# Score matmuls over all 128 rows, scratch in operand order, and fewer transfers in a two-layer encoder on one core

## The chip, the core and the metric

The kernel runs on one NeuronCore of one Trainium2 chip. The metric is the device time of one execution in microseconds. The kernel before takes 1938.34 us in the median of three runs (1934.69 to 1938.78). TensorE (PE) multiplies, its weight loads are shown as a row of their own (PEld), VectorE is DVE, ScalarE is ACT, GpSimd is POOL, and SyncE (SP) issues nearly all DMA transfers.

## What is computed

Two layers over 512 tokens of 1024 channels, in float32. Each layer has a mixer and a gated feed-forward part, each between two RMS norms:

```python
h = rms_norm(x, norm_mix_pre[l], NORM_EPS)
z = h @ w_in                                  # all q, k, v and the gates
# differential attention: 4 heads of two 64-wide score halves
s = einsum('bqhcd,bkhcd->bhcqk', qblk, kk) * scale
p = softmax(s); a = p[:, :, 0] - lam_full * p[:, :, 1]
o = einsum('bhqk,bkhe->bqhe', a, v)           # v is 128 wide
# three groups of 8 heads, window and dilation (128,1), (512,4), (2048,16)
og, lg = dilated_window_attention(qg, kg, vg, dilation, side)
ob = sum over groups of softmax(lse) * og
m = (sigmoid(g_A) * (oa @ w_a) + sigmoid(g_B) * (ob @ w_b)) @ w_out
x = x + rms_norm(m, ...); x = x + rms_norm(swiglu(rms_norm(x, ...)), ...)
```

q and k are rotated (rotary embedding over the two 32-wide halves of a 64-wide head) before the scores.

## The kernel before, in words

Activations are kept channel by token: `hT` holds the normed input as eight blocks of 128 channels by 512 tokens. Every float32 product is made of three matmuls of a rounded type: each operand is split into a high part and the rest (`mm3`, lines 123 to 125: high x high, low x high, high x low). Weights come in pieces of 1 MB (`load_raw`, line 90), two buffers of them; ACT rounds them (line 108) and DVE takes the rest (line 109).

TensorE's order is written out by hand. Projections are generators (`ws_gen`, `proj_v`) that give way after twelve matmuls over 512 columns, or 24 over 256; at each such point `att_step` emits one step of the attention work that is due. `attq` holds this work as a queue; a part is pushed when its projections are done, with a delay in steps (`DELAY`: 4 for the differential part, 7 for its first half; 4 for the first group, 2 for the others), and starts when the part ahead of it has issued its last scores. The heads of a layer are worked on in two halves (u = 0 and 1): first the differential part of both halves, then for each half the three dilated groups, then the gates and the output products. A step of attention has scores, some steps later transposes (line 521 or 646), and then products with v (line 532, 662 or 664), each for another item.

q and k leave the projection with the first rotary halves of four heads in one tile and the second halves in another, since the rotation needs them on the same rows. Scores need the 64 channels of a head on 64 rows. So `qk_split` writes the high and low parts to a scratch in DRAM (`dasc`) and reads them back in pieces of 32 rows. The three products of the high and low parts are two matmuls: QX holds for each head q's high part on 64 rows and its low part on the other 64 (which half is which alternates with the head), KX has k's high part twice, and KL k's low part, with two heads side by side on 128 rows:

```python
b = 64 * (c % 2)
nc.tensor.matmul(o, QX[:, c, qs], KX[:, c, ks], start=True, stop=False)
nc.tensor.matmul(o, QX[b:b + 64, c, qs], KL[b:b + 64, c // 2, ks], start=False, stop=True)
```

The second of them (line 488) works on 64 rows. The differential part and the first group use these two (512 and 256 columns); the second and third group take plain float32 operands from another scratch (`gsc`) with 64-row matmuls (line 616). The first group also moves v through DRAM (`vd`), because its windows need the tokens in natural order while the kernel keeps them by residue classes of 16; its result goes back through `scr` and `scs`. At the kernel's two ends x is read and written in that class order.

The transfers of q, k and v are all issued by SP, in one queue with the weight loads; an entry that waits holds up those behind it. `big` tiles (8 KB a row) have seven buffers, `m4` tiles eight.

Of the kernel before, what the change touches and what calls it, by code (L numbers as in the profile page):

```python
# [9 lines left out]
F32 = mybir.dt.float32  # L10
# [11 lines left out]
MOVE_POOL = 0  # L22
# [12 lines left out]
def encoder_trunk_kernel(  # L35
# [9 lines left out]
    mv = [0]  # L45
# [183 lines left out]
    def rows_in(xt, src, n, permuted):  # L229
        if permuted:  # L230
            for s in range(4):
                nc.sync.dma_start(out=xt[32 * s:32 * s + 32, :], in_=class_rows(src, n)[s])
        else:
            nc.sync.dma_start(out=xt, in_=src[n * P:(n + 1) * P, :])
# [17 lines left out]
    def postnorm_tile(n, pe, src, g, dst, src_perm, dst_perm):  # L252
# [12 lines left out]
        if dst_perm:  # L265
            for s in range(4):
                (nc.gpsimd if s == 3 else nc.sync).dma_start(out=class_rows(dst, n)[s], in_=xt[32 * s:32 * s + 32, :])
        else:
            nc.sync.dma_start(out=dst[n * P:(n + 1) * P, :], in_=xt)
# [51 lines left out]
    def specs():  # L321
# [11 lines left out]
        for l in range(depth):  # L333
            for u in range(2):
                yield from qkv(l, 256 * u, 512 + 256 * u, 1024 + 256 * u)[(1 if l == 0 and u == 0 else 0):]
            for u in range(2):
                for gi in range(3):
                    b = GB + gi * 1536 + 256 * u
                    yield from qkv(l, b, b + 512, b + 1024)
# [48 lines left out]
    for l in range(depth):  # L388
# [34 lines left out]
        def move(dst, src):  # L423
            mv[0] += 1
            eng = nc.gpsimd if MOVE_POOL and mv[0] % MOVE_POOL == 0 else nc.sync
            eng.dma_start(out=dst.bitcast(F32) if dst.dtype == F32R else dst,
                              in_=src.bitcast(F32) if src.dtype == F32R else src)

        def big(shape=(P, 4, S), dt=F32R):
            return ap.tile(list(shape), dt, tag="big", name=nm("big"), bufs=7)  # L430
# [25 lines left out]
        def qk_split(natural, first=None):  # L456
            QX, KX = big(), big()
            KL = m4([P, 2, S], F32R)
            sc = dp.tile([P, 2, 2, 2, S], F32, tag="dasc", name=nm("dasc"), bufs=2)
            for which in range(2):  # L460
                pair = rope((yield from proj_qk(which, first)), natural)
                hi = rt(F32R)
                nc.scalar.copy(out=hi, in_=pair)
                lo = rt(F32R)
                nc.vector.tensor_tensor(out=lo, in0=pair, in1=hi.bitcast(F32), op=ALU.subtract)
                move(sc[:, which, 0], hi)
                move(sc[:, which, 1], lo)
                src = sc.rearrange("(c j) w hl ab t -> w hl ab j c t", j=32)[which]
                if which == 0:
                    for hl in range(2):  # L470
# [429 lines left out]
```

## Time and profile before

| | |
|---|---|
| median of 3 runs | 1938.34 us |
| the profiled execution's own time | 1938.61 us |
| its span, first to last instruction | 1936.8 us |
| TensorE clock granted, mean | 0.994 |
| TensorE busy | 1889.4 us, 98% |
| weight loads busy | 1586.0 us, 82% |
| DVE, ACT, POOL busy | 929.5, 671.5, 179.9 us |
| DMA | 244.92 MB, 126 GB/s over the span |

A group row of the profile gives line, engine, operation, output<-inputs, shape and count, then busy time and mean duration, then the engine's idle time ahead of such instructions and what ended it. A time-line row starts with its start and its length in us, and in brackets stands the idle time before it with what ended it. A windows row gives the stretch, its length, the busy time of PE, PEld, DVE, ACT and POOL with their instructions, the granted TensorE clock, and DMA's busy share with GB/s. A transfer row gives the KB of each and the median us from issue to landing. The stages lie in time as follows: layer 0 has its differential scores from 79 us and its dilated groups until about 430 us, layer 1 the same from 1034 us and until about 1400 us; feed-forward parts lie behind each.

### The profile page before, as it was taken

Reading aid. Unit: us, or ns where it says so; the run is one execution under the profiler, and the core shown is the slowest. Engines: PE = TensorE matmul, PEld = TensorE weight load, DVE = VectorE, ACT = ScalarE, POOL = GpSimd, SP = SyncE. Lnnn points to the kernel's source line nnn. Section 1 sums busy time; section 2 is a strip of 40 time slices with the busy share of each in tenths; the row PEclk is TensorE's granted clock in tenths of the full one; section 3 lists DMA queues with packets and bytes.
Section 4 is the critical chain, followed back from the end, with each engine's and each line's share of the span. In section 5 each row is a group of like instructions: output and inputs, shape, how many; then the busy total and the mean of one; then the engine's idle time right before and its main releaser. Section 6 shows DMA issues by size and latency. Waiting matters only on the chain. (4 is left out here: it accounts for less than half of the span.)

```text
span 1936.8 us, 24393 instructions
## 1 busy us (share of the span) xinstructions
PE 1889.4 (98%) x9952; PEld 1586.0 (82%) x9952; DVE 929.5 (48%) x1243; ACT 671.5 (35%) x1301; POOL 179.9 (9%) x136
## 2 busy tenths in 40 slices
PE   6999999999999999999999999999999999999997
PEld 6878887888888888888887788878888888888886
DVE  4676556544545333332366765556453453333222
ACT  3354333344224322221334544323432342222221
POOL 1111013011100000000011211121100000000000
PEclk9999999999999999999999999999999999999999
DMA  6844446442244332322448254554323432323232
GB/s 176 253 127 131 121 120 185 129 121 87 87 163 153 109 109 87 103 94 88 162 151 233 88 151 120 151 162 130 100 89 137 144 131 89 107 87 109 87 119 65
DMA packets 171871, 244.92 MB, mean 126 GB/s; under 512 B 10864, under 2 KB 136176, under 8 KB 171760
## 3 DMA queue, kind: packets, MB, share of 16 engines
q1 hardware_dynamic: 171568, 242.84, 41.2%
q8 instruction: 78, 1.28, 0.3%
q0 software_dynamic: 192, 0.52, 0.1%
q14 instruction: 33, 0.27, 0.0%
HBM read 205.52 MB, written 37.81 MB: 126 GB/s over the span
## 5 line engine op out<-in xcount | busy, mean ns | idle before, releaser
L123 PE MATMUL pj<-hTh,whi 128*128 128x512 f32 (+1 forms) x1600 | 610.1, 381 | 3.0 <-ACT hTh L248 3.0
L124 PE MATMUL pj<-hTl,whi 128*128 128x512 f32 (+1 forms) x1600 | 600.2, 375 | 6.0 <-DVE hTl L249 5.9
L125 PE MATMUL pj<-hTh,wlo 128*128 128x512 f32 (+1 forms) x1600 | 599.6, 375 | 0.0
L109 DVE TENSOR_TENSOR wlo<-raw,whi 128x1024 fp32r<-128x1024 f32 x252 | 341.1, 1355 | 489.4 <-ACT whi L108 480.4
L108 ACT CAST whi<-raw 128x1024 fp32r<-128x1024 f32 x252 | 264.7, 1051 | 771.2 <-PE pj L124 498.6
L123 PEld LDWEIGHTS pj<-hTh,whi 128*128 128x128 f32 x1600 | 304.0, 190 | 62.7 <-ACT hTh L248 5.2
L124 PEld LDWEIGHTS pj<-hTl,whi 128*128 128x128 f32 x1600 | 304.3, 190 | 58.0 <-DVE hTl L249 7.7
L125 PEld LDWEIGHTS pj<-hTh,wlo 128*128 128x128 f32 x1600 | 304.1, 190 | 54.6
L123 PE MATMUL pj<-whi,hTh 128*128 128x256 f32 x512 | 148.5, 290 | 0.0
L125 PE MATMUL pj<-whi,hTl 128*128 128x256 f32 x512 | 144.8, 283 | 0.0
L124 PE MATMUL pj<-wlo,hTh 128*128 128x256 f32 x512 | 144.8, 283 | 0.0
L634 ACT ACTIVATE e<-e,gst 128x128 f32<-128x128 f32 (+1 forms) x192 | 81.9, 428 | 140.0 <-DVE gst L631 139.9
L77 POOL TENSOR_TENSOR sm<-sm,mhalf 128x1 f32<-128x1 f32 (+1 forms) x48 | 28.7, 599 | 970.1 <-DVE sm L75 970.1
L123 PEld LDWEIGHTS pj<-whi,hTh 128*128 128x128 f32 x512 | 97.9, 191 | 6.0 <-issue 3.7
L124 PEld LDWEIGHTS pj<-wlo,hTh 128*128 128x128 f32 x512 | 98.0, 191 | 0.0
L125 PEld LDWEIGHTS pj<-whi,hTl 128*128 128x128 f32 x512 | 98.0, 191 | 0.0
L825 DVE TENSOR_TENSOR s<-s,pj 128x512 f32<-128x512 f32 x44 | 30.3, 689 | 123.7 <-PE pj L125 123.6
L420 POOL TENSOR_TENSOR r<-r,r 128x512 f32<-128x512 f32 x32 | 43.0, 1344 | 453.3 <-DVE r L418 332.8
L418 DVE TENSOR_TENSOR r<-pj,cos 128x512 f32<-128x512 f32 x48 | 32.9, 690 | 77.4 <-PE pj L125 77.4
L419 POOL TENSOR_TENSOR r<-r,r 128x512 f32<-128x512 f32 x32 | 64.5, 2015 | 25.0 <-DVE r L418 25.0
L487 PE MATMUL at<-big,big 128*128 128x256 f32 (+1 forms) x128 | 55.3, 432 | 9.6 <-DMA vd<-m 7.5
L287 PE MATMUL pj<-whi,ac 128*128 128x512 f32 x160 | 63.0, 394 | 0.0
(166 smaller groups left out, 2482.0 us busy)
## 6 DMA issues: line engine op xcount, KB each, us to landing
raw<-in_w_in_dram SPq DMA_DIRECT2D x64, 1024.0 KB, 7.0
raw<-in_w_gate_up_dram SPq DMA_DIRECT2D x44, 1024.0 KB, 5.1
raw<-in_w_down_dram SPq DMA_DIRECT2D x22, 1024.0 KB, 4.8
dasc<-r SPq DMA_DIRECT2D x32, 512.0 KB, 3.5
big<-dasc SPq DMA_DIRECT2D x64, 128.0 KB, 6.6
big<-dasc SPq DMA_DIRECT2D x32, 256.0 KB, 8.0
gsc<-r SPq DMA_DIRECT2D x16, 512.0 KB, 3.5
big<-gsc SPq DMA_DIRECT2D x32, 256.0 KB, 7.3
```

Source lines behind the costliest of these rows:

```text
L108: nc.scalar.copy(out=shp(hi), in_=src)
L109: nc.vector.tensor_tensor(out=shp(lo), in0=src, in1=shp(hi.bitcast(F32)), op=ALU.subtract)
L123: nc.tensor.matmul(o, ah, bh, start=(i == 0), stop=False)
L124: nc.tensor.matmul(o, ah, bl, start=False, stop=False)
L125: nc.tensor.matmul(o, al, bh, start=False, stop=(i == n - 1))
L287: nc.tensor.matmul(o, al, hi[:, sl], start=False, stop=False)
L418: nc.vector.tensor_tensor(out=dst[:, i], in0=u, in1=tb, op=ALU.mult)
L419: nc.gpsimd.tensor_tensor(out=pair[:, 0], in0=pair[:, 0], in1=tmp[:, 0], op=ALU.subtract)
L420: nc.gpsimd.tensor_tensor(out=pair[:, 1], in0=pair[:, 1], in1=tmp[:, 1], op=ALU.add)
L487: nc.tensor.matmul(o, QX[:, c, qs], KX[:, c, ks], start=True, stop=False)
L634: nc.scalar.activation(out=e[:, i, :], in_=e[:, i, :], func=AF.Exp, bias=sts[:, n, h:h + 1], accum_out=sts[:, n, 4 + h:5 + h])
L825: nc.vector.tensor_tensor(out=s, in0=s, in1=ou_[i], op=ALU.mult)
```

## The change

- The low part of k gets a layout of its own, KL, over 128 rows. The scratch `dasc` now holds one of q or k with rows in the order (high or low, rotary half, channel), four heads beside each other, so that one read of 128 rows x 8 KB gives QX, one gives KH (high above low), and two of 64 rows give KL, the same halves swapped. Both score matmuls then use all 128 rows: QX x KH gives high x high and low x low, QX x KL the two mixed products. So a fourth product, low x low, is computed that was left out before.
- Each of q and k is written by four transfers of 256 KB and read by one (q) or three (k), where two writes and eight reads stood. The scratch has three buffers instead of two, `big` eight instead of seven.
- In the first group the order of the projections is k, v, q instead of q, k, v (the weight stream's order with it); the differential part and the other groups keep q, k, v.
- In the other two groups q's and k's halves are read back apart, each by one transfer; `vd`, `scr`, `scs`, the x rows at the start and the output rows at the end go by one transfer in place of four. The last output rows are all issued by SP; POOL had one in four.
- The number of score matmuls, their columns and the attention steps are as before. The DMA scratch space for POOL's transfers is set to 4096 bytes.

```diff
@@ -227,11 +225,7 @@
         return t.rearrange("(t s r) c -> r s t c", s=4, r=4)[n]
 
     def rows_in(xt, src, n, permuted):
-        if permuted:
-            for s in range(4):
-                nc.sync.dma_start(out=xt[32 * s:32 * s + 32, :], in_=class_rows(src, n)[s])
-        else:
-            nc.sync.dma_start(out=xt, in_=src[n * P:(n + 1) * P, :])
+        nc.sync.dma_start(out=xt, in_=class_rows(src, n) if permuted else src[n * P:(n + 1) * P, :])
 
     def prenorm_scale(xt, t, g):
         ss = small(1)
@@ -262,11 +256,7 @@
         nc.vector.tensor_tensor(out=ss, in0=ss2[:, 0:1], in1=ss2[:, 1:2], op=ALU.add)
         r = rstd_of(ss, 1, 1.0 / D, NORM_EPS)
         nc.vector.scalar_tensor_tensor(out=xt, in0=t, scalar=r, in1=xt, op0=ALU.mult, op1=ALU.add)
-        if dst_perm:
-            for s in range(4):
-                (nc.gpsimd if s == 3 else nc.sync).dma_start(out=class_rows(dst, n)[s], in_=xt[32 * s:32 * s + 32, :])
-        else:
-            nc.sync.dma_start(out=dst[n * P:(n + 1) * P, :], in_=xt)
+        nc.sync.dma_start(out=class_rows(dst, n) if dst_perm else dst[n * P:(n + 1) * P, :], in_=xt)
         return xt, t
 
     def new_hT():
@@ -336,7 +326,8 @@
             for u in range(2):
                 for gi in range(3):
                     b = GB + gi * 1536 + 256 * u
-                    yield from qkv(l, b, b + 512, b + 1024)
+                    q, k, v = qkv(l, b, b + 512, b + 1024)
+                    yield from (k, v, q) if gi == 0 else (q, k, v)
 
             def gates(c):
                 return [win(l, ZC + 256 * c, "cols"), win(l, ZC + D + 256 * c, "cols")]
@@ -421,13 +412,11 @@
             return pair
 
         def move(dst, src):
-            mv[0] += 1
-            eng = nc.gpsimd if MOVE_POOL and mv[0] % MOVE_POOL == 0 else nc.sync
-            eng.dma_start(out=dst.bitcast(F32) if dst.dtype == F32R else dst,
+            nc.sync.dma_start(out=dst.bitcast(F32) if dst.dtype == F32R else dst,
                               in_=src.bitcast(F32) if src.dtype == F32R else src)
 
         def big(shape=(P, 4, S), dt=F32R):
-            return ap.tile(list(shape), dt, tag="big", name=nm("big"), bufs=7)
+            return ap.tile(list(shape), dt, tag="big", name=nm("big"), bufs=8)
 
         oaT = [big() for i in range(2)]
 
@@ -453,43 +442,33 @@
                 nc.scalar.copy(out=v[:, 2 * n2:2 * n2 + 2, :], in_=o)
             return v
 
-        def qk_split(natural, first=None):
-            QX, KX = big(), big()
-            KL = m4([P, 2, S], F32R)
-            sc = dp.tile([P, 2, 2, 2, S], F32, tag="dasc", name=nm("dasc"), bufs=2)
-            for which in range(2):
-                pair = rope((yield from proj_qk(which, first)), natural)
-                hi = rt(F32R)
-                nc.scalar.copy(out=hi, in_=pair)
-                lo = rt(F32R)
-                nc.vector.tensor_tensor(out=lo, in0=pair, in1=hi.bitcast(F32), op=ALU.subtract)
-                move(sc[:, which, 0], hi)
-                move(sc[:, which, 1], lo)
-                src = sc.rearrange("(c j) w hl ab t -> w hl ab j c t", j=32)[which]
-                if which == 0:
-                    for hl in range(2):
-                        for ab in range(2):
-                            for par in range(2):
-                                o = 64 * ((hl + par) % 2) + 32 * ab
-                                move(QX[o:o + 32, par::2, :], src[hl, ab, :, par::2, :])
-                else:
-                    for ab in range(2):
-                        for o in (32 * ab, 64 + 32 * ab):
-                            move(KX[o:o + 32], src[0, ab])
-                        for par in range(2):
-                            o = 64 * par + 32 * ab
-                            move(KL[o:o + 32], src[1, ab, :, par::2, :])
-            return QX, KX, KL
+        def split_part_of(which, dsts, natural, first=None):
+            pair = rope((yield from proj_qk(which, first)), natural)
+            sc = dp.tile([P, 4, S], F32, tag="dasc", name=nm("dasc"), bufs=3)
+            rows = sc.rearrange("(hl ab j) c t -> hl ab c j t", hl=2, ab=2)
+            hi = rt(F32R)
+            nc.scalar.copy(out=hi, in_=pair)
+            for ab in range(2):
+                move(rows[0, ab], hi[:, ab, :])
+            lo = rt(F32R)
+            nc.vector.tensor_tensor(out=lo, in0=pair, in1=hi.bitcast(F32), op=ALU.subtract)
+            for ab in range(2):
+                move(rows[1, ab], lo[:, ab, :])
+            move(dsts[0], sc)
+            if len(dsts) > 1:
+                move(dsts[1][0:64], sc[64:128])
+                move(dsts[1][64:128], sc[0:64])
 
         def qk_scores(o, qk, c, qs, ks):
-            QX, KX, KL = qk
-            b = 64 * (c % 2)
-            nc.tensor.matmul(o, QX[:, c, qs], KX[:, c, ks], start=True, stop=False)
-            nc.tensor.matmul(o, QX[b:b + 64, c, qs], KL[b:b + 64, c // 2, ks], start=False, stop=True)
+            QX, KH, KL = qk
+            nc.tensor.matmul(o, QX[:, c, qs], KH[:, c, ks], start=True, stop=False)
+            nc.tensor.matmul(o, QX[:, c, qs], KL[:, c, ks], start=False, stop=True)
 
         def da_proj(first):
-            qk = yield from qk_split(False, first)
-            return qk, (yield from proj_v())
+            QX, KH, KL = big(), big(), big()
+            yield from split_part_of(0, (QX,), False, first)
+            yield from split_part_of(1, (KH, KL), False, first)
+            return (QX, KH, KL), (yield from proj_v())
 
         def da_attn(u, qk, v):
             items = [(n, h) for n in range(NT) for h in range(2)]
@@ -570,25 +549,24 @@
 
         def g_proj(gi):
             if gi == 0:
-                QK = yield from qk_split(True)
+                QX, KH, KL = big(), big(), big()
+                yield from split_part_of(1, (KH, KL), True)
                 v = yield from proj_v()
                 vd = dp.tile([S, 256], F32, tag="vd", name=nm("vd"), bufs=2)
-                for s in range(4):
-                    move(vd.rearrange("(t s r) c -> s t r c", s=4, r=4)[s], v[32 * s:32 * s + 32])
+                move(vd.rearrange("(t s r) c -> s t (r c)", s=4, r=4), v.rearrange("p r c -> p (r c)"))
                 vn = m4([P, NT, 256])
                 move(vn, vd.rearrange("(n p) c -> p n c", p=P))
                 vs = m4([P, 3, 256])
                 move(vs, vd[64:448].rearrange("(n p) c -> p n c", p=P))
-                return QK, vn, vs
+                yield from split_part_of(0, (QX,), True)
+                return (QX, KH, KL), vn, vs
             QK = big((P, 2, 2, S), F32)
-            sc = dp.tile([P, 2, 2, S], F32, tag="gsc", name=nm("gsc"), bufs=2)
             for which in range(2):
-                move(sc[:, which], rope((yield from proj_qk(which, None)), False))
-            src = sc.rearrange("(pair par j) w ab t -> par ab j w pair t", par=2, j=32)
-            for par in range(2):
+                pair = rope((yield from proj_qk(which, None)), False)
+                sc = dp.tile([P, 2, S], F32, tag="gsc", name=nm("gsc"), bufs=3)
                 for ab in range(2):
-                    o = 64 * par + 32 * ab
-                    move(QK[o:o + 32], src[par, ab])
+                    move(sc.rearrange("(pj ab) pair t -> ab pair pj t", ab=2)[ab], pair[:, ab, :])
+                move(QK[:, which], sc)
             return QK, (yield from proj_v()), None
 
         def g_attn(gi, QK, v, vs, res):
@@ -677,9 +655,8 @@
             move(scr.rearrange("(n p) c -> p n c", p=P), o)
             move(scs.rearrange("(n p) c -> p n c", p=P), st)
             oc, sc = g_out(0)
-            for s in range(4):
-                move(oc[32 * s:32 * s + 32], scr.rearrange("(t s r) c -> s t r c", s=4, r=4)[s])
-                move(sc[32 * s:32 * s + 32], scs.rearrange("(t s r) c -> s t r c", s=4, r=4)[s])
+            for dst, src in ((oc, scr), (sc, scs)):
+                move(dst.rearrange("p r c -> p (r c)"), src.rearrange("(t s r) c -> s t (r c)", s=4, r=4))
             return oc, sc
 
         def combine(u, res):
@@ -883,7 +860,7 @@
     from concourse import mybir as _mybir
     from concourse.bass_utils import run_bass_kernel_spmd as _run
 
-    nc = _bacc.Bacc("TRN2", target_bir_lowering=False, num_devices=1)
+    nc = _bacc.Bacc("TRN2", target_bir_lowering=False, num_devices=1, dynamic_dma_scratch_size=4096)
     arrays, args = {}, []
     named = [(n, inputs[n]) for n in _INS] + list(_constants().items())
     for name, value in named:
```

Where instructions now stand, at three places. The first is SP's queue at the first dilated group of the second half in layer 0 (`r` is the rotated q or k and its parts; `raw` a weight piece; `m` in the first listing is KL, in the row with `vd` it is v; `big` are QX and KX, or QX, KH and KL). Before:

```order
L426 DMA dasc_2598<-r_2712 128x1024
L426 DMA dasc_2598<-r_2714 128x1024
L426 DMA big_2595<-dasc_2598 32x2x512 x8
L426 DMA dasc_2598<-r_2831 128x1024
L426 DMA dasc_2598<-r_2833 128x1024
L90 DMA raw_2990<-in_w_in_dram 128x8x256
L426 DMA big_2596<-dasc_2598 32x4x512 x2
L426 DMA m_480_2597<-dasc_2598 32x2x512 x2
L426 DMA big_2596<-dasc_2598 32x4x512 x2
L426 DMA m_480_2597<-dasc_2598 32x2x512 x2
L426 DMA vd_2979<-m_527_2855 32x1024 x4
L426 DMA gsc_2989<-r_3069 128x1024
```

With the change:

```order
L415 DMA dasc_2671<-r_2672 4x32x512 x2
L415 DMA dasc_2671<-r_2676 4x32x512 x2
L415 DMA big_2556<-dasc_2671 128x2048
L415 DMA big_2557<-dasc_2671 64x2048 x2
L415 DMA vd_2831<-m_513_2693 4x32x1024
L88 DMA raw_2939<-in_w_in_dram 128x8x256
L415 DMA m_525_2833<-vd_2831 128x4x256
L415 DMA m_526_2835<-vd_2831 128x3x256
L88 DMA raw_3030<-in_w_in_dram 128x8x256
L415 DMA dasc_2928<-r_2929 4x32x512 x2
L415 DMA dasc_2928<-r_2933 4x32x512 x2
L415 DMA big_2555<-dasc_2928 128x2048
```

Before, the two writes of q, its reads, then k, then v, then the next group's q (`gsc`). Now k's writes and reads, v's write, a weight piece, v's reads, another weight piece, and q's writes and its one read as the last.

The second is TensorE's queue for the same group, where its last projection ends and the second group's q begins (`pj` is the projection's sum). Before:

```order
L124 MATMUL pj_2929<-wlo_2733,hTh_73 128x256
L125 MATMUL pj_2929<-whi_2732,hTl_74 128x256
L123 MATMUL pj_3000<-hTh_73,whi_2847 128x512
L124 MATMUL pj_3000<-hTl_74,whi_2847 128x512
L125 MATMUL pj_3000<-hTh_73,wlo_2848 128x512
```

With the change:

```order
L122 MATMUL pj_2848<-hTl_74,whi_2689 128x512
L123 MATMUL pj_2848<-hTh_73,wlo_2690 128x512
L121 MATMUL pj_2949<-hTh_73,whi_2839 128x512
L122 MATMUL pj_2949<-hTl_74,whi_2839 128x512
L123 MATMUL pj_2949<-hTh_73,wlo_2840 128x512
```

Before, the last projection was v's (its 24 matmuls at a time over 256 columns, with `hT` as the second operand); now it is q's, over 512 columns, whose result must still be rotated and go through the scratch. 48 matmuls of the second group's q follow in both.

The third is TensorE's queue behind these 48, at the first scores of the group (`at` is the score tile). Before:

```order
L125 MATMUL pj_3001<-hTh_73,wlo_2852 128x512
L714 MATMUL at_3050<-ident,m_440_2297 128x128 x4
L487 MATMUL at_3059<-big_2596,big_2595 128x256
L488 MATMUL at_3059<-m_480_2597,big_2595 128x256
L487 MATMUL at_3059<-big_2596,big_2595 128x256
L488 MATMUL at_3059<-m_480_2597,big_2595 128x256
L123 MATMUL pj_3088<-hTh_73,whi_2992 128x512
```

With the change:

```order
L123 MATMUL pj_2950<-hTh_73,wlo_2844 128x512
L691 MATMUL at_2999<-ident,m_443_2261 128x128 x4
L464 MATMUL at_3008<-big_2556,big_2555 128x256
L465 MATMUL at_3008<-big_2557,big_2555 128x256
L464 MATMUL at_3008<-big_2556,big_2555 128x256
L465 MATMUL at_3008<-big_2557,big_2555 128x256
L121 MATMUL pj_3040<-hTh_73,whi_2941 128x512
```

The scores stand at the same place behind the same transposes of the merged heads of the first half; the second matmul of each pair takes its moving operand from a `big` tile of 128 rows, where it was the 64 rows of an `m` tile.

More of the change, by code (lines that the diff above doesn't have):

```diff
@@ L21 @@
 SPLIT_PRI = 400
-MOVE_POOL = 0
 DELAY = (4, 4, 2, 2, 3)
@@ L44, in encoder_trunk_kernel @@
     depth = w_in.shape[0]
-    mv = [0]
     pp = ctx.enter_context(tc.tile_pool(name="pp", bufs=1))
```

## The prediction

> **What bounds the kernel now.** I read the page first, then the time line of TensorE where the score matmuls run, then the waits, then the transfers behind them.
>
> ```profile
> PE 1889.4 (98%) x9952; PEld 1586.0 (82%) x9952; DVE 929.5 (48%) x1243; ACT 671.5 (35%) x1301; POOL 179.9 (9%) x136
> L123 PEld LDWEIGHTS pj<-hTh,whi 128*128 128x128 f32 x1600 | 304.0, 190 | 62.7 <-ACT hTh L248 5.2
> ```
>
> TensorE is busy for 98% of the span, so only its own stream can be shortened. Busy time hides the pace, though: the durations in the time line are modelled, and the next matmul overlaps a part of each. The pace is the distance from start to start:
>
> ```profile
> 78.44 0.39 PE L125 MATMUL pj<-hTh,wlo 128*128 128x512 f32 x1
> 78.66 0.40 PE L487 MATMUL at<-big,big 128*128 128x512 f32 x1
> 78.99 0.49 PE L488 MATMUL at<-m,big 64*128 64x512 f32 x1
> 79.41 0.49 PE L487 MATMUL at<-big,big 128*128 128x512 f32 x1
> 79.83 0.50 PE L488 MATMUL at<-m,big 64*128 64x512 f32 x1
> 80.26 0.50 PE L123 MATMUL pj<-hTh,whi 128*128 128x512 f32 x1
> 80.60 0.39 PE L124 MATMUL pj<-hTl,whi 128*128 128x512 f32 x1
> 80.83 0.40 PE L125 MATMUL pj<-hTh,wlo 128*128 128x512 f32 x1
> ...
> 224.81 0.36 PE L487 MATMUL at<-big,big 128*128 128x256 f32 x1
> ...
> 226.03 0.39 PE L123 MATMUL pj<-whi,hTh 128*128 128x256 f32 x1
> 226.26 0.28 PE L124 MATMUL pj<-wlo,hTh 128*128 128x256 f32 x1
> 226.38 0.28 PE L125 MATMUL pj<-whi,hTl 128*128 128x256 f32 x1
> ```
>
> Projections over 512 columns start 0.22 to 0.23 us apart and those over 256 columns 0.12, each with its own weights: a load of 190 ns fits under the matmul before it. Where a matmul over 64 rows (L488) alternates with one over 128 (L487), the steps are 0.33, 0.42, 0.42 and 0.43, and the projection behind them takes 0.34. The reader is to see that every change of the row count costs 0.1 us or more, on both sides of L488, and that none of it stands in a list of waits.
>
> The second loss is two waits for scratch data, each with a lower clock after it:
>
> ```profile
> 331.68 0.35 PE L487 MATMUL at<-big,big 128*128 128x256 f32 x1 [3.55 <-DMA vd<-m]
> 1285.68 0.55 PE L487 MATMUL at<-big,big 128*128 128x256 f32 x1 [3.92 <-DMA vd<-m]
> 332.15:338.98 6.83, 6.83 (x17) 4.94 (x17) 1.38 (x2) 1.09 (x4) 0.12 (x1) 0.50 0.82 232
> 1284.47:1291.30 6.83, 5.62 (x13) 3.98 (x14) 3.25 (x4) 1.09 (x4) 2.40 (x2) 0.50 0.69 206
> 280.00:331.00 51.00, 45.78 (x282) 39.82 (x282) 36.83 (x50) 18.78 (x50) 15.45 (x8) 1.00 0.53 154
> L616 PE MATMUL at<-big 64*128 64x128 f32 x256 | 20.4, 286 | 3.4 <-DMA big<-gsc 3.3
> ```
>
> In the windows the granted clock stands third from the end: 0.50 for 6.83 us at each long wait. The stretch from 280 to 331, which holds the longest of the 3.3 us of waits for the second and third groups' operands (1.8 us at 281.6), kept 1.00.
>
> **The change, part by part.** *Score matmuls over 128 rows.* In the differential part two heads' scores, and in the first dilated group two blocks', are four matmuls in a row.
>
> ```profile
> L488 PE MATMUL at<-m,big 64*128 64x512 f32 x64 | 31.9, 498 | 0.0
> L488 PE MATMUL at<-m,big 64*128 64x256 f32 x64 | 25.1, 392 | 0.0
> 174.60 1.06 PE L532 MATMUL at<-m,e 128*128 128x128 f32 x8
> 175.49 0.60 PE L521 MATMUL at<-ident,e 128*128 128x128 f32 x4
> 175.85 0.48 PE L123 MATMUL pj<-hTh,whi 128*128 128x512 f32 x1
> ...
> 178.70 1.05 PE L532 MATMUL at<-m,e 128*128 128x128 f32 x8
> ```
>
> 64 and 64 of L488 make 32 fours of each width. Over 512 columns a four takes 80.26 - 78.66 = 1.60 us; at the projections' pace 4 x 0.227 = 0.91; the projection behind it gives back 0.34 - 0.23 = 0.11: 0.80 saved, x 32 = 25.6. Over 256 columns it takes 226.03 - 224.81 = 1.22; new 4 x 0.12 and the 0.11 that twelve projections, too, pay behind transposes (2.85 against 12 x 0.228), 0.59; behind it 0.23 - 0.12 = 0.11: 0.74, x 32 = 23.7. Together 49. Bounds: nothing if the row count isn't the cause, 49 if it is. I take 49: the nearest rows, projections with the same types, sizes and new weights each, run at that pace.
>
> [...]
>
> *Order k, v, q and larger transfers in the first group.* The two old waits end: 3.55 + 3.92 = 7.5 us, and half of two times 6.83 at half clock = 6.8. But q's round trip through the scratch is now the last. Its chain can be read where the first group's q of the second half stands now:
>
> ```profile
> 288.33 1.16 PE L616 MATMUL at<-big 64*128 64x128 f32 x16
> 293.16 1.05 ACT L463 CAST r<-r 128x1024 fp32r<-128x1024 f32 x1 [3.85 <-POOL r L419]
> 292.02 0.37 SPq L90 DMA_DIRECT2D raw<-in_w_in_dram  x1
> 294.23 1.60 SPq L426 DMA_DIRECT2D dasc<-r  x2
> 299.33 3.63 SPq L426 DMA_DIRECT2D big<-dasc  x8
> dasc<-r SPq DMA_DIRECT2D x32, 512.0 KB, 3.5
> raw<-in_w_down_dram SPq DMA_DIRECT2D x22, 1024.0 KB, 4.8
> raw<-in_w_in_dram SPq DMA_DIRECT2D x64, 1024.0 KB, 7.0
> ```
>
> The projection ends at 288.3, where L616 follows it. Rope and the rounded copy (L463) take until 294.2; the high part's write goes out then, behind a weight load, as in the new queue; its reads start when it has landed, at 299.3. The low part, issued 1.26 us later (1.60 for both, 0.34 of it the second issue), lands near 300.6, and two more issues of such a size make it 301.0 (eight take 3.63): 12.7 us after the projection. Then one read of 1 MB, which the trace does not show from the scratch. A weight load of that size takes 4.8 us with little beside it and 7.0 in company; I take 4.8, since the queue holds nothing else just then. So q is ready after 17.5 us, 19.7 at most by these rows, and 15.9 if the write takes the usual 3.5 instead of 5.1.
>
> What TensorE has meanwhile: in the second half 48 projection matmuls, 10.9, and four transposes, 0.4 (175.85 - 175.49): 11.3, so it waits 6.2 (4.6 to 8.4). In the first half the differential attention still drains there: 48 matmuls with their surcharges 11.2, three value products of 0.89 (175.49 - 174.60), two blocks of transposes of 0.36 and three small ones of 0.2: 15.2, so it waits 2.3 (0.7 to 4.5). For two layers 12.4 + 4.6 = 17.0. The longer wait is above the 3.55 that dropped the clock, so 6.8 come back; the shorter is nearer to the 1.8 that did not, and I take none for it.
>
> v's two transfers now have q's projection over them; without that cover they would be what the first score waits for, and the 7.5 would stay. k reads 2 MB instead of 1.5, under v and q in the first group and under v in the differential part, where also eight reads of nearly half a microsecond of issue each become one: nothing.
>
> *Second and third groups.* q's half is read early, k's in one transfer: the 3.3 us before L616 go.
>
> *Start, end, DVE.*
>
> ```profile
> 9.42 1.28 DVE L240 SCALAR_TENSOR_TENSOR m<-m,sm,m 128x1024 f32<-128x1024 f32 x1 [3.21 <-DMA m<-in_x_dram]
> 1930.92 1.28 DVE L264 SCALAR_TENSOR_TENSOR m<-m,sm,m 128x1024 f32<-128x1024 f32 x1 [1.72 <-DMA m<-xs]
> 138.00:162.00 24.00, 23.87 (x134) 18.39 (x133) 20.66 (x39) 13.30 (x32) 4.22 (x3) 1.00 0.47 125
> ```
>
> Three issues fewer ahead of the gain row (0.45 each) bring the first tile some 1.4 us forward (0 to the 3.2 waited). At the end the last x tile is asked for ahead of the third tile's store: the 1.7 us go, and one issue, 0.4: 2.1. Against that stands DVE: in one stretch of each layer it has 20.66 us of work in 24.00, and TensorE gives up four times 0.80 there. That leaves 20.8, so DVE would be full and queues form; I take 3 us for both layers, between 0 and the whole 6.4.
>
> Sum: 49.3 + 7.5 + 6.8 + 3.3 + 1.4 + 2.1 = 70.4 gained; 17.0 + 6.8 + 3 = 26.8 given back; 43.6 net. The profiled execution took 1938.6 us (its span 1936.8, and 1.8 around it), the median of the runs is 1938.3: **1895 us**. With the bounds of the waits, of the clock in the first half and of DVE it runs from 1886 to 1914.
>
> **The rivals.** *q is hidden after all*, its chain and read being quicker: 70.4 - 3 gained, 1871. For it: the transfers fill only half the time (0.53 in the stretch from 280 to 331). Against it: the chain up to the landed write alone takes 12.7, above the 11.3 of cover. *One more weight load stands ahead of q in the queue*: 4.8 more in four places, and the clock drops in the two others as well: 1895 + 19 + 7 = 1921. *DVE bounds the whole differential part*, not one stretch: half of the 25.6 is lost, 1908. *The row count isn't the cause*: the pace stays, 1938.6 - 21.1 + 23.8 = 1941; that L488 is slow on both its sides, and only its rows differ from L487's, speaks against it. *Slower*: the sync engine's queue. It issues in order, and q's writes stand behind weight loads that wait for DVE. With three loads more ahead of q (14.4 us) it is ready after 31.9: waits of 20.6 and 16.7, twice each, 74.6, with 13.6 of clock and the 3 of DVE against 70.4: 21 slower, 1959. It decides from two loads on; the new order puts only one there.
>
> **How the numbers follow.** Forecast 0.60, q hidden 0.10, one load more 0.12, DVE 0.08, row count 0.05, slower 0.05. A measurement of this kernel can tell 0.2% (3.9 us) from no change; 1941 falls within it. So 0.90 faster, 0.05 the same, 0.05 slower. The range takes in the forecast's own span, the hidden case up to its edge and the case of one load more: 1871 to 1922.
>
> **What would show it.** Right: score matmuls 0.23 and 0.12 us apart; waits of TensorE ahead of the first group's first score, longer in the second half and with a clock of 0.50 behind it; no wait for the scratch before the other groups' scores. Wrong: an unchanged pace of 0.42 or 0.31; a wait of over 8.4 us there, or none; score matmuls that wait for DVE or ACT all through the differential part.

## The result and the profile after

The changed kernel takes 2017.3 us in the median against 1938.1 for the kernel before: 1.0408 times as long, 95% interval 1.0388 to 1.0428. It is 79 us slower; 43 us faster was forecast. The profiled execution took 2016.43 us, its span is 2014.7 and the mean granted clock 0.968 (0.994 before).

The page of the changed kernel: the first row has each engine's busy time, the second the chain of work that ended last, by engine. After the change line 464 is the first score matmul (487 before), 465 the second (488), 594 the other groups' scores (616), 240 the transposes of the normed input (246), and 415 the line that issues scratch transfers (426).

```profile
PE 1856.3 (92%) x9952; PEld 1588.5 (79%) x9952; DVE 928.1 (46%) x1243; ACT 670.7 (33%) x1301; POOL 178.0 (9%) x132
PE 67%; DMA 9%; issue 3%; DVE 3%; POOL 1%; ACT 1%; SPq 1%; ACTq 0%; POOLq 0%; DVEq 0%
```

TensorE has 33 us less work than before and a span 78 us longer; DMA now holds 9% of the chain. The waits of TensorE, and then those of SP's queue, in the changed kernel (total, times, longest, all in us but the times):

```profile
PE at L464 <- DMA big<-dasc: 78.0, 6, 20.9
PE pj L240 <- DVE m L234: 22.6, 2, 17.7
PE at L240 <- DVE m L234: 9.3, 1, 9.3
PE at L465 <- DMA big<-dasc: 6.3, 2, 3.3
...
SPq L415 <- DMA dasc<-r: 164.3, 25, 11.1
SPq L415 <- DMA gsc<-r: 147.7, 16, 11.3
```

Six waits for the operands of the first scores add up to 78 us: four in the first group (10.7 us in the first half and 20.8 in the second, in both layers) and two at the start of the differential part (8.0 and 7.0). SP stands 147.7 us for the writes of the second and third groups, which carry the same bytes as before but are cut otherwise. Where one of the six comes from is seen in the time line of the changed kernel, TensorE first, then SP's queue, and in the windows of two stretches of it (length, five engines, granted clock, DMA's busy share, GB/s):

```profile
356.62 0.60 PE L691 MATMUL at<-ident,m 128*128 128x128 f32 x4
378.04 0.55 PE L464 MATMUL at<-big,big 128*128 128x256 f32 x1 [20.82 <-DMA big<-dasc]
...
354.52 6.80 SPq L415 DMA_DIRECT2D dasc<-r  x4
372.38 0.34 SPq L415 DMA_DIRECT2D big<-dasc  x1
372.81 1.06 SPq L415 DMA_DIRECT2D gsc<-r  x2
...
362.00:371.00 9.00, 0.00 (x0) 0.00 (x0) 0.00 (x0) 0.00 (x0) 0.23 (x1) 0.50 0.26 100
378.00:380.00 2.00, 1.96 (x7) 1.79 (x8) 0.69 (x2) 0.00 (x0) 0.00 (x0) 0.50 0.13 51
```

From 362 to 371 hardly anything runs but q's four writes (`dasc<-r`), and the 16 DMA engines are busy for 0.26 of the time with 100 GB/s: 0.26 x 16 is the work of a little over 4 engines. At 378 to 380 the next group's writes (`gsc<-r`) run alone: 0.13 x 16 is that of 2 engines, 51 GB/s. By estimate from these, 100 / 4 and 51 / 2, about 25 GB/s go through each engine in use, and the write's target is a view of 4 x 32 x 512 elements in the first case and 2 x 64 x 512 in the second. Before the change, the same data went out as 128 rows; the stretch that holds such a write behind a weight load (294 to 300) kept DMA at 0.86 and 312 GB/s:

```profile
294.00:300.00 6.00, 5.25 (x28) 4.18 (x27) 5.69 (x11) 4.10 (x16) 0.00 (x0) 1.00 0.86 312
```

The two ends show the same. TensorE's first matmul, and its wait for the third x tile, in the changed kernel, then the last two output stores in SP's queue and a window over them:

```profile
17.67 1.97 PE L240 MATMUL pj<-ident,m 128*128 128x128 f32 x8 [17.67 <-DVE m L234]
44.25 1.12 PE L240 MATMUL at<-ident,m 128*128 128x128 f32 x4 [9.32 <-DVE m L234]
...
1997.43 6.78 SPq L259 DMA_DIRECT2D out_dram<-m  x2
...
1997.00:2006.00 9.00, 0.05 (x1) 0.00 (x0) 3.10 (x6) 0.69 (x2) 0.55 (x1) 0.69 0.26 101
```

The first matmul starts at 17.67 (10.76 before), and with the stores of whole tiles, 4 x 32 x 1024, DMA again stands at 0.26.

The shares of 0.26 and 0.13, taken of 16, go with views whose slowest dimension is 4 and 2. The author's reading is that such a view is carried by as many engines; the profile gives the shares, not the engines one by one.

### The profile page after: what moved, and what is told of

It reads as the page before. It is cut to its first block, busy times and chain, and to the rows that moved or that the text cites. A ratio compares the mean times of both kernels' runs of the same rounds, so it can differ in the third digit from the quotient of the medians.

```text
span 2014.7 us, 24172 instructions
## 1 busy us (share of the span) xinstructions
PE 1856.3 (92%) x9952; PEld 1588.5 (79%) x9952; DVE 928.1 (46%) x1243; ACT 670.7 (33%) x1301; POOL 178.0 (9%) x132
## 4 chain that ended last, share of the span: by engine, by line
PE 67%; DMA 9%; issue 3%; DVE 3%; POOL 1%; ACT 1%; SPq 1%; ACTq 0%; POOLq 0%; DVEq 0%
PE pj L121 16%; PE pj L122 16%; PE pj L123 16%; DMA dasc<-r 4%; PE pj L276 2%; PE pj L277 2%; PE pj L278 2%; PE at L277 2%; PE at L276 2%; PE at L278 2%; DMA raw<-in_w_in_dram 2%; DMA big<-dasc 1%; PE at L640 1%; PE at L642 1%; PE at L624 1%
## 5 line engine op out<-in xcount | busy, mean ns | idle before, releaser
L121 PEld LDWEIGHTS pj<-hTh,whi 128*128 128x128 f32 x1600 | 308.3, 193 | 58.6 <-ACT hTh L242 5.1
L464 PE MATMUL at<-big,big 128*128 128x256 f32 (+1 forms) x128 | 50.9, 407 | 81.4 <-DMA big<-dasc 78.0
L464 PEld LDWEIGHTS at<-big,big 128*128 128x128 f32 x128 | 25.6, 200 | 90.1 <-issue 63.9
L607 DVE TENSOR_TENSOR e<-at,mk 128x512 f32<-128x512 f32 x64 | 42.9, 680 | 66.3 <-PE at L465 65.9
```

Of the source, the lines that this page charges most:

```text
L121: nc.tensor.matmul(o, ah, bh, start=(i == 0), stop=False)
L464: nc.tensor.matmul(o, QX[:, c, qs], KH[:, c, ks], start=True, stop=False)
L607: nc.vector.tensor_tensor(out=e, in0=o, in1=mask, op=ALU.add)
```

## The experiments

Theory A is that reading: the transfers that were cut anew run on 4 or 2 engines, and what waits for them is late. Theory B is that q, last in its group and read only when all its writes have landed, is late whatever the engines do. Theories C and D take up what A leaves.

**All cuts undone.** Each of these transfers is cut so that its slowest dimension is 32 or 64; order, layouts, whole reads and 128-row scores stay.

```diff
-            rows = sc.rearrange("(hl ab j) c t -> hl ab c j t", hl=2, ab=2)
+            rows = sc.rearrange("(hl ab j) c t -> hl c j ab t", hl=2, ab=2)
-            for ab in range(2):
-                move(rows[0, ab], hi[:, ab, :])
+            for c in range(4):
+                move(rows[0, c], hi[32 * c:32 * c + 32])
...
-                for ab in range(2):
-                    move(sc.rearrange("(pj ab) pair t -> ab pair pj t", ab=2)[ab], pair[:, ab, :])
+                for pr in range(2):
+                    move(sc.rearrange("(pj ab) pair t -> pair pj ab t", ab=2)[pr], pair[64 * pr:64 * pr + 64])
... (lo like hi; vd, scr, scs, x rows, output rows in pieces of 32 rows, as before the change)
```

> The changed kernel with each re-cut transfer cut so that its slowest dimension is 32 or 64 instead of 4 or 2 (x and output rows, v, to-class rows in four pieces of 32 as before the change; the scratch writes by column group or pair). Order, operands, layouts and the one-transfer reads stay as changed. Theory A (a transfer whose slowest dimension is 4 or 2 runs on 4 or 2 of the 16 DMA engines, and everything that waits for it is late): the waits of TensorE for the scratch, 78.0 us in the changed kernel, fall to the 17 that the prediction gave or less, the half-clock windows behind them go, the first matmul comes at 10 to 11 us instead of 17.7: 1880 to 1910 us. Theory B (the round trip is long because q is last and the reads are whole transfers that start only when all four writes have landed, whatever engines they run on): the waits stay over 60 us, 1985 to 2010 us.

Measured: 1943.3 us, ratio to before 1.003 (1.0018 to 1.0041). The cuts are worth 74 us of the 79, but neither theory's figure came: the waits for the scratch are still 49.1 us in four places, all in the first group. Waits, a window over q's eight writes in the second half of layer 0 (with v's reads and a weight load among them), SP's queue in the first half, and TensorE there and in the second half (in this kernel line 472 is the first score matmul, 423 the scratch line):

```profile
PE at L472 <- DMA big<-dasc: 49.1, 4, 13.1
PE at L472 <- ACT e L510: 4.9, 14, 0.7
PE at L472 <- DVE big L546: 4.3, 2, 2.2
PE at L472 <- ACT e L495: 2.3, 4, 0.8
...
322.50:331.50 9.00, 5.48 (x27) 4.33 (x25) 4.30 (x6) 0.59 (x1) 2.49 (x2) 1.00 0.79 247
...
173.82 4.43 SPq L423 DMA_DIRECT2D dasc<-r  x8
187.31 1.22 SPq L423 DMA_DIRECT2D gsc<-r  x2
188.76 0.49 SPq L423 DMA_DIRECT2D big<-dasc  x1
...
196.30 0.58 PE L472 MATMUL at<-big,big 128*128 128x256 f32 x1 [13.08 <-DMA big<-dasc]
339.73 0.58 PE L472 MATMUL at<-big,big 128*128 128x256 f32 x1 [11.75 <-DMA big<-dasc]
```

With the wider cuts DMA is at 0.79 and 247 GB/s, where q's writes ran at 0.26 and 100. In the first half q's eight writes are issued by 178.3 and have landed by 183 (DMA moves nothing from there until 186.01), but its read goes out at 188.76: two writes of the next group, which wait for that group's rotation, stand ahead of it in SP's queue. In the changed kernel the read stood ahead of them.

**Only the scratch writes cut again.** The edit is the part of the diff above that is shown; x, output, v and to-class transfers stay whole.

> Only the scratch writes of q and k (first group, differential part, second and third groups) cut so that the slowest dimension is 32 or 64; x rows, output rows, v and the to-class reads stay whole, on 4 engines. Theory A: of the 107 to 137 us that the re-cut of everything would bring, the start (7.0), the end (7.6) and the two waits for late x tiles (22.6 and 9.3 in the list of waits) stay; v's write stays at some 10 us but has q's projection over it: 15 to 40 us above the kernel with everything cut again, 1905 to 1945 us. Theory B: 1985 to 2017 us.

Measured: 1981.5 us, ratio 1.0232 (1.0214 to 1.025). So, undone in this order, 35.8 us of the slowdown belong to the scratch writes, and 38.2 to x, output, v and the way back to class order. The second figure is within what theory A said of it; the total is not, since that counted on 1895 for the rest.

**x and output rows whole, in the kernel before.** This is the change's smallest part, done alone.

```diff
-            for s in range(4):
-                nc.sync.dma_start(out=xt[32 * s:32 * s + 32, :], in_=class_rows(src, n)[s])
+            nc.sync.dma_start(out=xt, in_=class_rows(src, n))
... (output rows likewise, one store on SP; POOL had one piece in four)
```

> The kernel before with one edit: each tile of x rows is loaded, and each tile of output rows stored, in one transfer over the permuted rows (slowest dimension 4) instead of four pieces of 32 rows. Theory A: start some 7 us later, the third and fourth x tile late by 9 to 22, end 7 to 8 later, in the first layer's output part another wait for x: 14 to 40 us slower, 1952 to 1978 us. Theory B, by which the number of issues sets these times: 1 to 4 us faster, 1934 to 1937 us.

Measured: 1973.3 us, ratio 1.0186 (1.0171 to 1.0201): theory A. With three issues in four saved it is 36 us slower. TensorE's waits in this kernel, for x tiles:

```profile
PE pj L242 <- DVE m L236: 23.1, 2, 17.6
PE at L242 <- DVE m L236: 8.6, 1, 8.6
```

**Only the slowest dimension.** In the changed kernel the two writes of a second- or third-group projection are split the other way, as in the second half of the first diff. Their number, their bytes and their pieces of 2 KB stay.

> The changed kernel with one edit: the two writes of each second- and third-group projection to the scratch are split by pair of heads instead of by half of the rotary pair. Number of transfers (2), bytes (256 KB each), pieces (2 KB) and target addresses as a whole stay the same; only the slowest dimension is 64 instead of 2. Theory A (that dimension sets the number of engines): such a write falls from 11 us or so to 4 or less, as in the kernel with everything cut again (3.7), the share of the DMA engines during it is no longer 2/16 = 0.13, SP's waits for these writes (147.7 us) fall under 70, the four waits of 2.4 to 2.6 before the other groups' scores go: 1980 to 2008 us. Theory E (2 KB pieces scattered over the scratch are slow by themselves): the writes still take 10 us or more, 2010 to 2018 us.

Measured in one execution: 2003.1 us, 14 less than the changed kernel. SP's waits for these writes in this kernel:

```profile
SPq L415 <- DMA gsc<-r: 52.6, 16, 4.8
```

They were 147.7, the longest 11.3. Number, bytes and pieces are the same; what differs is which dimension comes first (and with it that a write takes 64 whole rows of the tile, not half of each of 128 rows). So it is that, not scattered pieces of 2 KB.

**64 rows in the second score matmul.** All cuts undone, with

```diff
-            nc.tensor.matmul(o, QX[:, c, qs], KL[:, c, ks], start=False, stop=True)
+            nc.tensor.matmul(o, QX[0:64, c, qs], KL[0:64, c, ks], start=False, stop=True)
```

> As the kernel with everything cut again, but the second score matmul uses rows 0 to 63 only (high part of q by low part of k; the product of q's low part with k's high part is left out). Same number of matmuls, same columns, same transfers. If the change of the row count costs 0.1 us or more at each switch, as the prediction says: 35 to 55 us above the kernel with everything cut again, with starts 0.42 and 0.31 apart. [...]

Measured: 1990.7 us, ratio 1.0281 (1.0264 to 1.0297), 47.4 more than with 128 rows. The same four matmuls in the time line, first with 128 rows throughout, then with 64 in the second (line 473):

```profile
76.36 0.39 PE L472 MATMUL at<-big,big 128*128 128x512 f32 x1
76.59 0.40 PE L473 MATMUL at<-big,big 128*128 128x512 f32 x1
76.82 0.39 PE L472 MATMUL at<-big,big 128*128 128x512 f32 x1
77.05 0.39 PE L473 MATMUL at<-big,big 128*128 128x512 f32 x1
77.28 0.39 PE L121 MATMUL pj<-hTh,whi 128*128 128x512 f32 x1
...
80.52 0.40 PE L472 MATMUL at<-big,big 128*128 128x512 f32 x1
80.85 0.50 PE L473 MATMUL at<-big,big 64*128 64x512 f32 x1
81.28 0.50 PE L472 MATMUL at<-big,big 128*128 128x512 f32 x1
81.71 0.50 PE L473 MATMUL at<-big,big 64*128 64x512 f32 x1
```

Starts are 0.23 apart in the first and 0.33 to 0.43 in the second. Over 256 columns, at full clock, the four start 0.12 apart with 128 rows (in the changed kernel from 226.76 us on). The row count is the cause.

**The read ahead of the next group's writes.** All cuts undone, and in SP's queue the second group's first writes and one weight load are kept behind q's read:

```diff
+                with tc.issue_after(last_read[0].ins):
                     for pr in range(2):
                         move(sc.rearrange("(pj ab) pair t -> pair pj ab t", ab=2)[pr], pair[64 * pr:64 * pr + 64])
... (the same around this group's v projection, for its weight load)
```

> As the kernel with everything cut again, but in SP's queue the read of the first group's q in the first half stands ahead of the second group's first scratch writes and of one weight load; it stood behind them, 8.5 us after q's writes had landed (180.1, issue at 188.8). Nothing else is moved in the queue. If that place in the queue is the cause of the wait of 13.1 us: it falls to 3 to 6 us in both layers, the half-clock windows behind it get shorter: 15 to 30 us faster, 1913 to 1928 us. If the transfers' own time is the cause: 1938 to 1944 us. The wait of 11.8 us in the second half stays in either case.

Measured: 1920.1 us, ratio 0.9897 (0.9879 to 0.9915). The place in the queue was the cause of the first half's wait: of 13.08 us, 1.93 stay. TensorE's first scores of both halves in layer 0, its waits, and SP's queue in the second half (line 474 is the first score matmul here; the wait put down to `gsc<-r` is that of layer 1's second half, at the same matmul):

```profile
186.26 0.35 PE L474 MATMUL at<-big,big 128*128 128x256 f32 x1 [1.93 <-DMA big<-dasc]
329.96 0.58 PE L474 MATMUL at<-big,big 128*128 128x256 f32 x1 [11.99 <-DMA big<-dasc]
...
PE at L474 <- DMA big<-dasc: 15.3, 3, 12.0
PE at L474 <- DMA gsc<-r: 11.5, 1, 11.5
...
312.47 1.18 SPq L425 DMA_DIRECT2D dasc<-r  x2
313.84 0.97 SPq L425 DMA_DIRECT2D m<-vd  x2
315.18 3.24 SPq L425 DMA_DIRECT2D dasc<-r  x6
318.46 0.44 SPq L88 DMA_DIRECT2D raw<-in_w_in_dram  x1
321.92 0.34 SPq L425 DMA_DIRECT2D big<-dasc  x1
```

**The old order of projections.** All cuts undone, the first group projects q, k, v.

```diff
-                    yield from (k, v, q) if gi == 0 else (q, k, v)
+                    yield from (q, k, v)
... (g_proj: split_part_of(0, ...) ahead of split_part_of(1, ...), v last)
```

> As the kernel with everything cut again (1943 us), but the first dilated group projects q, k, v in the old order; whole reads, 128-row scores and cuts stay. The remaining waits there are four for the read of q: 49.1 us, with 51.2 us at half clock behind them, which cost some 25.6. Theory C (what is left is the order: q last has only the delay of four steps, 10.9 us, over its round trip): these go, and some 7 to 15 us come back for the data that are last now (v, or k's three reads with v's projection over them): 1875 to 1895 us. Theory D (the whole reads themselves are late, 1 MB after the last of the writes): k's reads, now late in the same way, make TensorE wait over 8 us in each of the four places: 1915 to 1945 us.

Measured: 1914.8 us, ratio 0.9867 (0.9846 to 0.9888): 20 us above theory C's figure, at the lower edge of theory D's. The four waits for q are gone, and 13.2 us for the scratch stay, none longer than 4.6, where theory D had over 8 in each of four places:

```profile
PE at L473 <- DMA big<-dasc: 9.1, 3, 4.6
PE at L472 <- DMA big<-dasc: 4.1, 2, 2.4
```

The waits went as theory C has it; its figure did not come. 1943.3 less 49.1, with 13.2 back, is 1907.4, so most of the error is the 25.6 us that it took for the half clock behind the waits, which is taken up below; some 7 us stay open.

**A longer delay.** All cuts undone, order k, v, q with nine steps, and order q, k, v with seven.

```diff
-DELAY = (4, 4, 2, 2, 3)
+DELAY = (4, 9, 2, 2, 3)
... (in the kernel with the old order: 7 in place of 9)
```

> As the kernel with everything cut again, but the first group's attention starts nine steps of twelve matmuls after its last projection instead of four (13.7 us more projections ahead of its first scores); order k, v, q. Theory C (the round trip lacks cover, nothing else): all four waits go, and the 51 us of half clock with them: 1866 to 1882 us. Rival: the attention that starts later lacks projections at the end of each half, or the groups' operands hold each other's buffers, and the wait only moves: over 1920 us.

> The old order q, k, v in the first group, everything cut again, whole reads, 128-row scores, and a delay of seven steps instead of four. Theory C: no wait for the scratch is left: 1863 to 1880 us, faster than the kernel before by 3 to 4% and faster than the same kernel with a delay of four by 5 to 20. Theory D: the waits get shorter by 8 us each only, 1900 us or more.

Measured: 1919.3 us, ratio 0.9891 (0.9876 to 0.9906), and 1925.7, ratio 0.9922 (0.9907 to 0.9937). Theory C's figure failed in both, by 37 us and more. For seven steps theory D's "1900 us or more" came, but not as it has it: of the 13.2 us for the scratch 0.4 are left. In the kernel with nine steps the scratch is no longer waited for in the first group, but TensorE has waits that the one with four had not:

```profile
PE at L603 <- DVE e L634: 11.1, 8, 2.0
PE pj L122 <- DVE wlo L107: 8.8, 2, 4.4
```

The delayed steps now fall together with the next groups' work: scores of these wait for a copy of transposed scores by DVE, and a projection waits for DVE to round its weights. With the old order seven steps cost 11 us more than four.

**Order made by the reads, and the combine on DVE.** In the kernel with the old order, q and k are written as they stand, and each operand is read in four pieces; then the combine's two POOL operations go to DVE, in that kernel and in the one with whole reads.

```diff
+            move(sc[:, 0], hi)
...
+                        move(d[o:o + 32], rows[(part + first_half) % 2, ab])
...
-                (nc.gpsimd if i == 0 else nc.vector).tensor_tensor(out=ov, in0=ov, in1=wv, op=ALU.mult)
-            nc.gpsimd.tensor_tensor(out=os_[0], in0=os_[0], in1=os_[1], op=ALU.add)
+                nc.vector.tensor_tensor(out=ov, in0=ov, in1=wv, op=ALU.mult)
+            nc.vector.tensor_tensor(out=os_[0], in0=os_[0], in1=os_[1], op=ALU.add)
```

> As the kernel with the old order q, k, v and everything cut again (1914.8 us), but q and k are written to the scratch as they stand (two transfers over 128 rows, high and low part, as before the change), and the operand order is made by four reads of 32 rows for each operand. Scores over 128 rows stay. In that kernel the eight writes of k in the second half take from 305.3 to 314.7 to land, its three reads until 324.9, and TensorE waits 6.5 and 6.3 us for them, once in each layer. If the eight issues and the wait for all of them are what is late: writes land by 310, reads by 320, these 12.8 us fall to 4 or less: 1900 to 1909 us. If the 3 MB of a projection's traffic are: no change, 1911 to 1918 us.

> As the kernel with writes as they stand and reads in order, but the two POOL operations that combine the three groups at the end of each half (2.55 and 3.36 us) run on DVE. In the kernel with the old order k's rope in the second half stands behind them on POOL until 300.7, and begins 3 us later than its DVE part allows. If that delays the scores: 2 to 8 us faster than without this edit. If DVE, which has 10.5 us of work in 11 there, is the next bound: 0 to 5 us slower.

> The fastest kernel so far (everything cut again, old order q, k, v, writes in operand order and whole reads: 1914.8 us) with the combine's two POOL operations on DVE. In the kernel with reads in order this edit gave 4.7 us. If the rope of k that stands behind them on POOL is what makes the first scores of the second half wait 6.5 and 6.3 us: the waits shrink by 2 to 3 each, 1907 to 1912 us. If the waits are the transfers' own: 1913 to 1917 us.

Measured: 1922.0 (ratio 0.9915, 0.9898 to 0.9933), 1917.3 (0.9895, 0.9879 to 0.991) and 1907.6 us (0.9839, 0.9818 to 0.986). Plain writes with reads in pieces are 7 us worse than writes in operand order with whole reads (9 by the ratios), against both branches of the expectation: once its cuts are wide, that part of the change is the better way. Moving the combine gave 4.7 us in one kernel and, set against the kernel before each time, 0.28% of it (5 us) in the other. TensorE's waits for the scratch in the last kernel, 13.2 us with the combine on POOL:

```profile
PE at L473 <- DMA big<-dasc: 8.6, 3, 4.1
```

In the second half of layer 0, from the start of v's projection, which follows k's, to k's first write it is now 8.0 us (297.28 to 305.28), and was 10.2 (295.13 to 305.31). This bears out the expectation that k's rotation stood behind the combine on POOL; the intervals of the two ratios overlap in each pair, so the size of the gain isn't settled. The last kernel beats both the kernel before, by 1.6%, and the changed one, by 110 us.

## Why the prediction was wrong

**Score matmuls over 128 rows: right.** Forecast 49.3, measured 47.4 by the kernel with 64 rows. The pace is the projections' pace, 0.23 and 0.12. This also decides the rival in which the row count is not the cause.

**Order k, v, q and larger transfers: the step that failed.** It took "5.1" us for the high part's write from a row of 128 x 1024, and "two more issues of such a size make it 301.0". The writes kept their bytes but not their form, and the bytes were all that was priced. In the changed kernel q's write goes out at 354.52 and its read can start at 372.38, 17.9 us later, where the prediction had 6.8. For k's "2 MB instead of 1.5" the prediction had "nothing": in the changed kernel the first scores of the differential part wait 8.0 and 7.0 us for the scratch, and with all cuts undone not at all. The 3.3 us before the other groups' scores were to go: in the changed kernel 4.9 us are waited for `gsc` there, and with all cuts undone none, so that term was right but for the form of the writes. Together the form of the scratch writes cost the 35.8 us.

With the cuts undone, the chain is still longer than forecast. In the kernel whose read is in place, the rotation and ACT's copy end at 312.45 and the first write is issued at 312.47; the read goes out at 321.92, once the last of eight has landed (9.5 us, 6.8 forecast), and with the whole read, 1 MB behind a weight load issued at 318.46, the scores start at 329.96 (8.0 us, 4.8 forecast). The way from the end of the projection to the first write was as forecast (from about 306.6, 5.9 us). So the second half waits 12.0 us, not 6.2. The first half waits 1.93, where 2.3 were forecast: there the step was right, once the queue was.

**The slower rival was half seen.** It put the fault into SP's queue, with weight loads ahead of q. In the changed kernel q's read did not stand behind such an entry. The 13.1 us with the cuts undone did come from that queue, but from the next group's scratch writes, which wait for the rotation. The order of issue by itself did not tell how long an entry would stand there.

**Start and end: the sign was wrong.** The gain of 1.4 and 2.1 counted issues. The same edits alone cost 36 us in the kernel before: one issue for four, but with DMA at 0.27 and 86 GB/s from 12 to 20 us and at 0.25 and 98 GB/s from 1955 to 1960, where the kernel before, with pieces of 32 rows, has 0.76 and 232 near its end (1927 to 1930.5).

**The clock: too dear behind long waits.** The prediction took 3.4 us for each of the two longer waits, half of a window of 6.83 at half clock; the expectations for the old order and for the longer delay took half of windows twice as long, 6.8 each. With all cuts undone, the 13.65 us at half clock around the first half's wait hold 3.36 us of TensorE work (second column, granted clock third from the end):

```profile
186.01:199.66 13.65, 3.36 (x10) 2.88 (x11) 1.86 (x4) 0.65 (x3) 1.27 (x1) 0.50 0.72 230
```

The rest of that window is the wait itself, so the half clock costs there by estimate 1.7 us at most, half of the 3.36. Between this kernel and the one with the read in place the waits for the first group's scores fall by 22.3 us and the time by 23.2 (25.8 by their ratios to the kernel before). On the other side of the sum the charge was nearly right: the windows behind the two old waits, 6.83 long, held 6.83 and 5.62 us of work.

**The differential part: too cheap.** With all cuts undone TensorE waits 11.5 us for ACT and DVE there (7.2 for ACT's exponentials and copies, lines 495 and 510, and 4.3 for DVE), where 1.7 stood before and 3 more were forecast, for DVE alone.

Added up, the changed kernel's 2017.3 us become 1943.3 without the narrow transfers and 1920.1 with the read in place. Of the 25 us from there to the forecast, 3.5 are the gains at start and end, which the pieces of 32 rows cannot make, 11 the waits of the second half (12.0 and 11.5 against 12.4 for both), and 7 the differential part; some 4 are not accounted for, as much as the kernel before differed between these two experiments (1936.8 and 1941.0 us). What makes that part wait for ACT and DVE was not tried.

## What to carry to other kernels

A transfer is priced by its form as well as its bytes: with the same bytes SP waited 147.7 us for one cut of the `gsc` writes and 52.6 for the other. Before several pieces are made one, look at the slowest dimension of the joined view, in a read and in a write: here a stretch with writes of 32 rows, v's reads and a weight load ran at 247 GB/s, while 4 and 2 left the writes at about 100 and 51 GB/s, and the shorter list of issues did not pay for that. When a stage's read is moved to the end of a chain, look for what now stands ahead of it in the issuing queue, and for how long that entry itself must wait.

## What was not expected of the hardware

The rate went with DMA's busy share: 51 GB/s with 0.13, and 100 with 0.26, from the same kernel and pieces of the same 2 KB. In the changed kernel the profile could no longer tell the time from issue to landing for any transfer, the wide ones included; the row of the weight loads, with its 7.0 us before the change, reads

```profile
raw<-in_w_in_dram SPq DMA_DIRECT2D x64, 1024.0 KB
```

No run here shows why.

The window of half clock lay mostly inside the long wait. A short wait of 3.55 us was followed by 6.83 us of work at half clock; one of 13.1 by a window of which 3.4 held work. So the second costs less clock than the first.
